# First modulation block requested earlier, convolution taps and small columns later, partial sums joined in PSUM, and each slab's matmuls issued in two halves

## The chip, the core and the metric

The kernel runs on one core of one Trainium2 chip. The time is that of the device in microseconds (us), from the first instruction of the program to the last; one launch does the whole computation. The engines named below are PE (TensorE matmuls; PEld is its weight load), DVE (VectorE), ACT (ScalarE), POOL (GpSimd) and SP (SyncE, which here only requests transfers). Each engine works through its own instructions in the order in which they stand in the program; a suffix q (SPq, ACTq) marks an engine's own queue handling, such as a request for a transfer.

## The reference, cut to what matters

One layer of a streaming encoder on x of shape 512 x 1024. What this study touches is the very beginning:

```
c_act = silu(c)                                   # c has 1024 numbers
mod   = c_act @ mod_w + mod_b                     # 1024 x 6144, split in six: sh1, sc1, g1, sh2, sc2, g2
h     = rms_norm(x, norm1_g) * (1 + sc1) + sh1    # 512 x 1024
proj  = h @ w_in                                  # 1024 x 8192, split among conv, HGRN2, stick-breaking, gates
```

Behind it come three branches (a causal convolution of 31 taps per channel, a gated linear recurrence, a stick-breaking attention), their gated sum, an output projection, a residual, and an MLP of width 4096 with squared ReLU. All inputs are float32.

## The kernel before, in words

Products are kept near float32 precision by splitting each operand in a high and a low part of the type float32r (`hilo`: ACT copies the high part, DVE subtracts it to get the low part) and by adding three matmuls (`mm3`, lines 113 to 115).

The first stage goes over the contraction dimension in eight steps j = 0 to 7, each for 128 rows of `w_in`. A step needs three things:

- **block(j)**, the tile `ms`: 128 columns of sc1 and 128 of sh1 from `mod_w`, 1 MB in two requests of 512 KB on SP (`load_ms`, line 130). `prep_mod` multiplies its eight row groups by c_act and adds them up in a tile `acc` of two halves: ACT makes the first product of each half (line 236), DVE adds the other six (line 238). For j > 0 DVE then joins the two halves (line 241); PE sums over the partitions with matmuls against a column of ones into the PSUM tile `tp` (line 245), and DVE makes from it the scale and shift of 128 channels (lines 247 and 248, the columns `modc`).
- **h(j)**: PE transposes 128 columns of the normalized x into the PSUM tile `tq` (line 254), ACT applies scale and shift (line 258, tile `s`) and copies the high part (line 83, tile `ht`), DVE makes the low part (line 84).
- **slab(j)**: 128 rows by 768 columns of `w_in` (`load_slab`, line 139), split into `fwh` and `fwl`.

Then `first_mm(j)` issues 18 matmuls into six PSUM tiles (`mm` and `f`), which are kept open over all eight steps. `prep(j)` stands ahead of `first_mm(j-1)` in the code.

Ahead of the loop, x comes in four tiles of 512 KB (line 143); each is squared and summed on ACT (line 88), and scaled by its reciprocal root on DVE (line 226). Small inputs come on ACT's queue: `vecs` (115 rows of 128 numbers: c, biases, gains) and `conv_w` (31 rows of 512, the **taps**), which PE transposes into columns (lines 170 and 175). Eight matmuls on constants (line 285) keep PE at work before the first real ones.

The order of the instructions on each engine is not that of the code: a scheduler, with its own estimate of how long things take, sets it when the program is built. `tc.issue_after(x)` forbids it to place what stands inside ahead of the instruction x.

Of the kernel before, what the change touches and what calls it, by code (L numbers as in the profile page):

```python
# [15 lines left out]
P = 128  # L16
# [5 lines left out]
CW = 31  # L22
# [16 lines left out]
def tile_hybrid_block(ctx, tc, x, vecs, mod_w, mod_b, w_in, conv_w, w_conv, w_hgrn, w_sb, w_out, w1, w2, out):  # L39
# [30 lines left out]
    def S(shape=(P, T), dt=F32, g=""):  # L70
        return spool.tile(list(shape), dt, name=TAG.get(g, "s"), bufs=BUFS.get(TAG.get(g)))
# [38 lines left out]
    def mm3(o, lhs, rhs, start, stop):  # L110
        lh, ll = lhs
        rh, rl = rhs
        TE.matmul(o, lhsT=lh, rhs=rh, start=start, stop=False)  # L113
        TE.matmul(o, lhsT=lh, rhs=rl, start=False, stop=False)  # L114
        TE.matmul(o, lhsT=ll, rhs=rh, start=False, stop=stop)  # L115


    vrow = S((NVEC, P), g="c0")
    A.dma_start(vrow, vecs)
    cw_row = S((CW, 512), g="c0")  # L120
    A.dma_start(cw_row, conv_w)
    x_v = x.rearrange("(a p) d -> a p d", p=P)
# [14 lines left out]
    def load_slab(j):  # L137
        slabs[j] = wpool.tile([P, W0], F32, name="slab", bufs=10)
        SY.dma_start(slabs[j], wi_row[:, j, C_A + 256:C_A + 256 + W0])

    for t in range(NT):
        xt.append(P4((P, D), g="x0"))
        SY.dma_start(xt[t], x_v[t])
    load_ms(0)
    load_slab(0)
# [26 lines left out]
    V.tensor_copy(vcol, vp[:, 0:NVEC])  # L172
    cp = ax()
    for i in range(4):
        TE.transpose(cp[:, i * 32:i * 32 + CW], cw_row[:, i * P:(i + 1) * P], ident[0:CW, 0:CW])
    cwc = C([P, 4, 32], F32)
    V.tensor_copy(cwc[:, :, 0:CW], cp[:, 0:128].rearrange("p (i k) -> p i k", k=32)[:, :, 0:CW])

    cact = C([P, 8], F32)
# [7 lines left out]
    oml = C([P, 4], F32)
    lb = vcol[:, V_HLB:V_HLB + 4]
    lbe = C([P, 4], F32)
    lbs = C([P, 4], F32)  # L190
    V.tensor_tensor(out=lbe, in0=lb, in1=lb, op=ALU.subtract)
    ph(lbe, lbe, AF.Exp)
    V.reciprocal(out=lbs, in_=lbe)
    V.tensor_tensor(out=lbe, in0=lbe, in1=lbs, op=ALU.mult)
    V.tensor_tensor(out=lbs, in0=lbe, in1=lbe, op=ALU.subtract)
    V.tensor_scalar(out=oml, in0=lbs, scalar1=-1.0, scalar2=1.0, op0=ALU.mult, op1=ALU.add)

    gbh = C([P, 24], F32)
    V.tensor_scalar(out=gbh, in0=vcol[:, V_GB:V_GB + 24], scalar1=0.5, scalar2=None, op0=ALU.mult)
    lnh = C([P, 8], F32)  # L200
    V.tensor_scalar(out=lnh, in0=vcol[:, V_LG:V_LG + 8], scalar1=0.5, scalar2=None, op0=ALU.mult)

# [7 lines left out]


    facc = [mm() if i < 4 else ps("f") for i in range(6)]
    hT, fw = [], {}

# [13 lines left out]
    def prep_mod(j):  # L228
        ms = ms_t.pop(j)
        acc = S((P, 2, 2, P), g="acc")  # L230
        for kk in range(KT):
            a, src, c = acc[:, kk % 2], ms[:, :, kk, :], cact[:, kk:kk + 1]
            if kk < 2 and j == 0:
                V.tensor_scalar(out=a, in0=src, scalar1=c, scalar2=None, op0=ALU.mult)
            elif kk < 2:
                A.activation(a, src, AF.Identity, scale=c)
            else:
                V.scalar_tensor_tensor(out=a, in0=src, scalar=c, in1=a, op0=ALU.mult, op1=ALU.add)
        ne = 2 if j == 0 else 1
        if ne == 1:  # L240
            V.tensor_tensor(out=acc[:, 0], in0=acc[:, 0], in1=acc[:, 1], op=ALU.add)
        tp = ps("tp")
        for q in range(2):
            for e in range(ne):
                TE.matmul(tp[:, q:q + 1], lhsT=acc[:, e, q, :], rhs=ones[:, 0:1], start=(e == 0), stop=(e == ne - 1))
        gs, sh = modc[:, j:j + 1], modc[:, 8 + j:9 + j]
        V.scalar_tensor_tensor(out=gs, in0=tp[:, 0:1], scalar=mb1[:, j:j + 1], in1=vcol[:, V_N1 + j:V_N1 + j + 1], op0=ALU.add, op1=ALU.mult)
        V.tensor_tensor(out=sh, in0=tp[:, 1:2], in1=vcol[:, V_MB + j:V_MB + j + 1], op=ALU.add)

    def prep_h(j):  # L250
# [17 lines left out]

    def prep(j):
        load_ms(j)  # L270
        load_slab(j)
        prep_mod(j)
        prep_h(j)
        prep_w(j)

    def first_mm(j):
        wh, wl = fw.pop(j)
        for i in range(6):
            c = slice(i * P, (i + 1) * P)
            mm3(facc[i], (wh[:, c], wl[:, c]), hT[j], j == 0, j == KT - 1)  # L280


    wu = ps("tq")
    for i in range(8):
        TE.matmul(wu, lhsT=ident, rhs=scanm.rearrange("p a t -> p (a t)"), start=True, stop=True)
    for t in range(NT):
        x_norm(t)
    prep_mod(0)
    prep_h(0)
    prep_w(0)  # L290
# [787 lines left out]
```

## Time and profile before

| | us |
|---|---|
| three runs, median (lowest to highest) | 924.02 (922.34 to 924.3) |
| the profiled execution, its own time | 924.09 |
| its span in the profile | 922.3 |
| first matmul of `first_mm(0)` begins | 25.06 |
| first matmul of step 4 begins | 47.13 |
| last matmul of step 7 begins | 65.79 |

The table's last three times count from the start of the span. PE is busy for 894.8 us of the 922.3. The busy time of PE is modelled (matmuls overlap), so a stretch with a full count can still hold short gaps.

### The profile page before, as it was taken

What the parts mean: (1) busy time and instruction counts of PE and PEld (TensorE: products, weight loads), DVE (VectorE), ACT (ScalarE), POOL (GpSimd) and SP (SyncE); (2) the same over time, 40 slices, a digit from 0 to 9 for tenths busy, and PEclk for the clock granted to TensorE, in tenths of its full rate; (3) what the DMA queues carried; (4) which work ended last, traced back from release to release, by engine and by line L of the source; (5) the groups of instructions that cost most, each with busy time, mean ns of one, the idle gap of its engine ahead of it and who ended that gap; (6) DMA issues with size and microseconds to landing.
All of it is one profiled execution on the core that took longest, in us unless ns stands there. A gap on an engine that the chain in (4) does not pass through costs nothing.

```text
span 922.3 us, 10624 instructions
## 1 busy us (share of the span) xinstructions
PE 894.8 (97%) x4185; PEld 728.8 (79%) x4185; DVE 599.5 (65%) x886; ACT 385.8 (42%) x596; POOL 28.1 (3%) x35
## 2 busy tenths in 40 slices
PE   4999989999988999999999999999999999999998
PEld 2788878888755588888888888888888888888886
DVE  4882388899999999997965544774423254442422
ACT  4652434475788632223833536453312123431210
POOL 1002000001032000000000000000000000000000
PEclk9999999999999999999999999999999999999999
DMA  9981301131200344793423620552242233142121
GB/s 279 279 268 59 113 12 46 52 132 46 91 1 1 115 159 162 245 329 136 138 86 103 216 70 1 192 196 91 92 137 92 56 113 106 46 137 92 68 69 46
DMA packets 85418, 107.78 MB, mean 117 GB/s; under 512 B 2270, under 2 KB 58705, under 8 KB 85368
## 3 DMA queue, kind: packets, MB, share of 16 engines
q1 hardware_dynamic: 85200, 106.96, 35.5%
q8 instruction: 33, 0.54, 0.3%
q14 instruction: 17, 0.14, 0.1%
q10 hardware_dynamic: 168, 0.14, 0.0%
HBM read 105.00 MB, written 2.10 MB: 116 GB/s over the span
## 4 chain that ended last, share of the span: by engine, by line
PE 88%; DVE 6%; ACT 3%; DMA 2%; issue 1%; SPq 1%; DVEq 0%; ACTq 0%
PE mm L113 14%; PE mm L114 14%; PE mm L115 14%; PE ax L115 9%; PE ax L113 9%; PE ax L114 9%; PE o L115 2%; PE o L114 2%; PE o L113 2%; PE g L113 2%; PE g L114 2%; PE g L115 2%; PE g L654 1%; DVE bt L545 1%; PE o L573 1%; DVE bt L546 1%
## 5 line engine op out<-in xcount | busy, mean ns | idle before, releaser
L84 DVE TENSOR_TENSOR wl<-w,wh 128x1024 fp32r<-128x1024 f32 x134 | 162.8, 1221 | 194.4 <-ACT wh L83 147.4
L83 ACT ACTIVATE wh<-w 128x1024 fp32r<-128x1024 f32 x134 | 139.8, 1054 | 290.8 <-PE ax L115 129.9
L113 PE MATMUL mm<-ht,wh 128*128 128x512 f32 x272 | 106.7, 392 | 0.0
L115 PE MATMUL mm<-ht,wl 128*128 128x512 f32 x272 | 106.6, 392 | 0.0
L114 PE MATMUL mm<-ht,wh 128*128 128x512 f32 x272 | 106.6, 392 | 0.0
L114 PE MATMUL mm<-p,wh 128*128 128x512 f32 (+1 forms) x272 | 102.6, 378 | 0.0
L115 PE MATMUL mm<-p,wl 128*128 128x512 f32 (+1 forms) x272 | 102.4, 377 | 0.0
L113 PE MATMUL mm<-p,wh 128*128 128x512 f32 (+1 forms) x272 | 102.3, 377 | 0.0
L462 DVE SCALAR_TENSOR_TENSOR cv<-cv,cbig 128x511 f32<-128x511 f32 (+29 forms) x120 | 83.5, 733 | 0.0
L113 PEld LDWEIGHTS mm<-ht,wh 128*128 128x128 f32 x272 | 51.1, 188 | 11.2 <-issue 0.8
L114 PEld LDWEIGHTS mm<-ht,wh 128*128 128x128 f32 x272 | 51.1, 188 | 11.0 <-issue 0.6
L115 PEld LDWEIGHTS mm<-ht,wl 128*128 128x128 f32 x272 | 51.1, 188 | 10.4 <-issue 0.2
L114 PEld LDWEIGHTS mm<-p,wh 128*128 128x128 f32 x272 | 51.2, 188 | 9.4
L115 PEld LDWEIGHTS mm<-p,wl 128*128 128x128 f32 x272 | 51.2, 188 | 9.4
L113 PEld LDWEIGHTS mm<-p,wh 128*128 128x128 f32 x272 | 51.0, 188 | 9.3
L113 PE MATMUL ax<-wh,p 128*128 128x512 f32 x128 | 49.8, 389 | 0.0
L114 PE MATMUL ax<-wl,p 128*128 128x512 f32 x128 | 49.8, 389 | 0.0
L115 PE MATMUL ax<-wh,p 128*128 128x512 f32 x128 | 49.8, 389 | 0.0
L113 PE MATMUL ax<-wh,s 128*128 128x512 f32 x128 | 49.8, 389 | 0.0
L114 PE MATMUL ax<-wl,s 128*128 128x512 f32 x128 | 49.8, 389 | 0.0
L115 PE MATMUL ax<-wh,s 128*128 128x512 f32 x128 | 49.8, 389 | 0.0
L865 DVE SCALAR_TENSOR_TENSOR s<-p,cbig,s 128x512 f32<-128x512 f32 x64 | 47.1, 746 | 1.5 <-DMA p<-in_mod_w_dram 1.2
(248 smaller groups left out, 1666.8 us busy)
## 6 DMA issues: line engine op xcount, KB each, us to landing
w<-in_w_dram SPq DMA_DIRECT2D x32, 1024.0 KB, 5.7
w<-in_w_in_dram SPq DMA_DIRECT2D x27, 1024.0 KB, 5.3
p<-in_mod_w_dram SPq DMA_DIRECT2D x32, 512.0 KB, 7.4
ms<-in_mod_w_dram SPq DMA_DIRECT2D x16, 512.0 KB, 5.9
w<-in_w_out_dram SPq DMA_DIRECT2D x4, 1024.0 KB
slab<-in_w_in_dram SPq DMA_DIRECT2D x8, 384.0 KB, 4.6
x<-in_x_dram SPq DMA_DIRECT2D x4, 512.0 KB, 8.9
w<-in_w_hgrn_dram SPq DMA_DIRECT2D x2, 1024.0 KB, 4.9
```

The lines of the kernel that those rows point to most:

```text
L83: A.activation(hi, src, AF.Copy)
L84: V.tensor_tensor(out=lo, in0=src, in1=hi.bitcast(F32), op=ALU.subtract)
L113: TE.matmul(o, lhsT=lh, rhs=rh, start=start, stop=False)
L114: TE.matmul(o, lhsT=lh, rhs=rl, start=False, stop=False)
L115: TE.matmul(o, lhsT=ll, rhs=rh, start=False, stop=stop)
L462: V.scalar_tensor_tensor(out=cacc[i][:, d:], in0=cu[i][:, 0:T - d], scalar=w, in1=cacc[i][:, d:], op0=ALU.mult, op1=ALU.add)
L545: V.tensor_tensor_scan(out=kp[:, 0:n][:, ::-1], data0=kp[:, 0:n][:, ::-1], data1=kp[:, 0:n][:, ::-1], initial=1.0, op0=ALU.mult, op1=ALU.b ...
L546: V.tensor_tensor(out=bt[:, 0:n - 1], in0=bt[:, 0:n - 1], in1=kp[:, 1:n], op=ALU.mult)
L573: TE.matmul(o[h * 64:h * 64 + 64, sb * P:T], lhsT=svt[sb][:, pr * P + h * 64:pr * P + h * 64 + 64], rhs=ahs[h][bi][:, off:off + n], start= ...
L654: TE.matmul(o[:, b * n:(b + 1) * n], lhsT=l, rhs=r, start=True, stop=True)
L865: V.scalar_tensor_tensor(out=a, in0=box["s"][:, kk, :], scalar=cact[:, 2 * k2 + kk:2 * k2 + kk + 1], in1=a, op0=ALU.mult, op1=ALU.add)
```

## The change

Five edits. `load_ms(0)` stands ahead of the requests for x in the code. The load of the taps, their transposes and the copy are put into `conv_columns`, called behind step 3's matmuls and not to be requested before line 265 of step 3 (`hb[3]`, the scale and shift of h(3)); other small columns are put into `lb_columns`, called behind step 1's. DVE no longer joins the halves of `acc` (line 241 is gone): PE adds both halves in PSUM, with four matmuls in place of two per step. `first_mm` is issued in two halves of three tiles, and `tp`, `tq` and all that follows for h(j) come between them, not to be issued before the first half has been. And `prep_w` comes ahead of `prep_h`.

```diff
-    cw_row = S((CW, 512), g="c0")
-    A.dma_start(cw_row, conv_w)
...
+    load_ms(0)
     for t in range(NT):
         xt.append(P4((P, D), g="x0"))
         SY.dma_start(xt[t], x_v[t])
-    load_ms(0)
     load_slab(0)
...
+    def conv_columns():
+        cw_row = S((CW, 512), g="c0")
+        with tc.issue_after(hb[3].ins):
+            A.dma_start(cw_row, conv_w)
+        cp = ax()
+        for i in range(4):
+            TE.transpose(cp[:, i * 32:i * 32 + CW], cw_row[:, i * P:(i + 1) * P], ident[0:CW, 0:CW])
+        V.tensor_copy(cwc[:, :, 0:CW], cp[:, 0:128].rearrange("p (i k) -> p i k", k=32)[:, :, 0:CW])
...
-        ne = 2 if j == 0 else 1
-        if ne == 1:
-            V.tensor_tensor(out=acc[:, 0], in0=acc[:, 0], in1=acc[:, 1], op=ALU.add)
+        return acc
+
+    def prep_sum(j, acc):
         tp = ps("tp")
         for q in range(2):
-            for e in range(ne):
-                TE.matmul(tp[:, q:q + 1], lhsT=acc[:, e, q, :], rhs=ones[:, 0:1], start=(e == 0), stop=(e == ne - 1))
+            for e in range(2):
+                TE.matmul(tp[:, q:q + 1], lhsT=acc[:, e, q, :], rhs=ones[:, 0:1], start=(e == 0), stop=(e == 1))
...
+    prep_sum(0, prep_mod(0))
     for t in range(NT):
         x_norm(t)
-    prep_mod(0)
+    prep_w(0)
     prep_h(0)
-    prep_w(0)
     for j in range(1, KT + 1):
         if j < KT:
-            prep(j)
-        first_mm(j - 1)
+            load_ms(j)
+            load_slab(j)
+            acc = prep_mod(j)
+            prep_w(j)
+        mid = first_mm(j - 1, range(3))
+        if j < KT:
+            with tc.issue_after(mid.ins):
+                prep_sum(j, acc)
+                prep_h(j)
+        first_mm(j - 1, range(3, 6))
+        if j == 2:
+            lb_columns()
+        if j == 4:
+            conv_columns()
```

What the scheduler makes of it at two places. **The start.** SP's first requests before (the four tiles of x are x_78 to x_84) and now (x_79 to x_85):

```order
L143 DMA x_78<-in_x_dram 128x1024
L143 DMA x_80<-in_x_dram 128x1024
L143 DMA x_82<-in_x_dram 128x1024
L143 DMA x_84<-in_x_dram 128x1024
L130 DMA ms<-in_mod_w_dram 128x8x128 x2
L139 DMA slab<-in_w_in_dram 128x768
```

```order
L142 DMA x_79<-in_x_dram 128x1024
L142 DMA x_81<-in_x_dram 128x1024
L142 DMA x_83<-in_x_dram 128x1024
L128 DMA ms<-in_mod_w_dram 128x8x128 x2
L142 DMA x_85<-in_x_dram 128x1024
L137 DMA slab<-in_w_in_dram 128x768
```

Block(0) has moved ahead of one tile of x, the last; three still stand ahead of it. On ACT, from the high part of slab(1) to that of slab(2), before (line 236 is a product of block(2), line 258 the scale and shift of h(0)) and now (lines 243 and 265):

```order
L83 ACTIVATE fwh<-slab 128x768
L258 ACTIVATE s<-tq,cbig 128x512
L236 ACTIVATE acc<-ms,cbig 128x256
L83 ACTIVATE ht<-s 128x512
L236 ACTIVATE acc<-ms,cbig 128x256
L83 ACTIVATE fwh<-slab 128x768
```

```order
L83 ACTIVATE fwh<-slab 128x768
L265 ACTIVATE s<-tq,cbig 128x512
L83 ACTIVATE ht<-s 128x512
L243 ACTIVATE acc<-ms,cbig 128x256 x2
L83 ACTIVATE fwh<-slab 128x768
```

The high part of h(0) no longer stands behind a product that needs block(2).

**Steps 3 and 4.** On ACT now, from the second product of block(5) ahead of h(3) on; the tile c_401 is the taps:

```order
L265 ACTIVATE s<-tq,cbig 128x512
L243 ACTIVATE acc<-ms,cbig 128x256
L83 ACTIVATE ht<-s 128x512
L83 ACTIVATE fwh<-slab 128x768
L100 ACT_TABLE_LOAD
L196 DMA c_401<-in_conv_w_dram 31x512
L243 ACTIVATE acc<-ms,cbig 128x256 x2
L265 ACTIVATE s<-tq,cbig 128x512
```

Before, the request of the taps was the second on ACT's queue (line 121), and no product stood between the lines 258 and 83 of h(1), h(2) or h(3), as line 243 does now in each. On PE now, from the sums of block(4) (which stand ten matmuls into step 3) to the first matmuls of step 4; line 199 transposes the taps:

```order
L252 MATMUL tp<-crs,acc 128x1 x4
L261 MATMUL tq<-crs,x_79 128x128
L261 MATMUL tq<-crs,x_81 128x128
L261 MATMUL tq<-crs,x_83 128x128
L261 MATMUL tq<-crs,x_85 128x128
L114 MATMUL mm<-ht,fwh 128x512
L115 MATMUL mm<-ht,fwl 128x512
L113 MATMUL f<-ht,fwh 128x512
L114 MATMUL f<-ht,fwh 128x512
L115 MATMUL f<-ht,fwl 128x512
```

```order
L113 MATMUL f<-ht,fwh 128x512
L114 MATMUL f<-ht,fwh 128x512
L115 MATMUL f<-ht,fwl 128x512
L199 MATMUL ax<-crs,c_401 128x31 x4
L113 MATMUL mm<-ht,fwh 128x512 x4
```

Behind the sums of block(4) come four transposes and eight matmuls of step 3, then the taps, then step 4. Before, the taps' transposes (line 175) were PE's second work, and the sums stood at the seam of two steps or a few matmuls into one. From the end of this stage on, all engines have the same instructions in the same order as before.

## Rows read from the trace of the kernel before

**Rows 1.** The page: busy time by engine (part 1), chain that ended last (part 4).

```profile
PE 894.8 (97%) x4185; PEld 728.8 (79%) x4185; DVE 599.5 (65%) x886; ACT 385.8 (42%) x596; POOL 28.1 (3%) x35
...
PE 88%; DVE 6%; ACT 3%; DMA 2%; issue 1%; SPq 1%; DVEq 0%; ACTq 0%
```

**Rows 2.** Stretches: length, PE, PEld, DVE, ACT, POOL busy, PE clock, DMA share, GB/s.

```profile
0.00:25.06 25.06, 11.49 (x37) 6.04 (x37) 11.48 (x38) 11.25 (x27) 3.70 (x17) 0.99 0.93 282
15.00:20.00 5.00, 5.00 (x14) 2.20 (x13) 5.00 (x14) 4.66 (x14) 0.00 (x0) 1.00 0.83 235
25.00:28.00 3.00, 2.94 (x8) 2.36 (x9) 1.43 (x3) 1.14 (x3) 0.00 (x0) 0.50 1.14 315
31.49:47.13 15.64, 15.64 (x85) 12.94 (x84) 14.89 (x38) 10.14 (x17) 0.00 (x0) 1.00 0.98 267
47.13:65.79 18.66, 18.62 (x91) 15.16 (x90) 17.42 (x44) 11.15 (x16) 0.00 (x0) 1.00 0.91 286
```

**Rows 3.** Chain that ended last, 25 to 66 us: shares by line.

```profile
by line: PE mm L113 21.4%; PE mm L114 18.7%; PE mm L115 18.5%; PE f L113 9.4%; PE f L115 8.9%; PE f L114 8.9%; PE tp L245 7.3%; PE tq L254 6.7%; ACT ht L83 1.3%; PE g L113 0.6%; issue 0.2%
```

**Rows 4.** Instructions in order of time, 0 to 25 us: start, length, ..., [idle before <-releaser].

```profile
0.73 0.56 ACTq L119 DMA_DIRECT2D c<-in_vecs_dram  x1
...
1.33 0.24 ACTq L121 DMA_DIRECT2D c<-in_conv_w_dram  x1
...
4.78 0.42 PE L170 MATMUL ax<-crs,c 115*128 115x115 f32 x1 [4.78 <-DMA c<-in_vecs_dram]
...
10.90 1.64 SPq L130 DMA_DIRECT2D ms<-in_mod_w_dram  x2
...
10.91 0.63 PE L175 MATMUL ax<-crs,c 31*128 31x31 f32 x4 [5.71 <-DMA c<-in_conv_w_dram]
...
14.43 0.35 DVE L234 TENSOR_SCALAR acc<-ms,cbig 128x256 f32<-128x256 f32 x1 [1.89 <-DMA ms<-in_mod_w_dram]
...
15.34 0.85 ACT L83 ACTIVATE fwh<-slab 128x768 fp32r<-128x768 f32 x1 [1.84 <-DMA slab<-in_w_in_dram]
...
19.88 0.95 PE L245 MATMUL tp<-crs,acc 128*128 128x1 f32 x8
...
22.71 0.78 ACT L258 ACTIVATE s<-tq,cbig 128x512 f32<-128x512 f32 x1 [2.04 <-DVE cbig L248]
...
23.98 0.51 ACT L236 ACTIVATE acc<-ms,cbig 128x256 f32<-128x256 f32 x1 [0.49 <-DMA ms<-in_mod_w_dram]
24.40 0.61 ACT L83 ACTIVATE ht<-s 128x512 fp32r<-128x512 f32 x1
...
25.06 2.07 PE L113 MATMUL mm<-ht,fwh 128*128 128x512 f32 x4 [2.63 <-ACT ht L83]
```

**Rows 5.** ACT's DMA queue, 5 to 6 us: packets, MB, share of 16 engines.

```profile
q10 hardware_dynamic: 4, 0.01, 2.1%
```

**Rows 6.** Instructions in order of time, steps 1 and 2 (columns as in Rows 4).

```profile
32.73 0.56 PE L245 MATMUL tp<-crs,acc 128*128 128x1 f32 x4
...
33.33 0.22 DVE L247 SCALAR_TENSOR_TENSOR cbig<-tp,cbig 128x1 f32<-128x1 f32 x1 [0.31 <-PE tp L245]
...
33.73 0.78 ACT L258 ACTIVATE s<-tq,cbig 128x512 f32<-128x512 f32 x1 [1.79 <-DVE cbig L248]
...
34.54 0.63 ACT L83 ACTIVATE ht<-s 128x512 fp32r<-128x512 f32 x1
...
39.46 1.28 ACT L100 ACT_TABLE_LOAD   x1
```

**Rows 7.** Groups by line, 31.45 to 61.65 us: busy us, mean ns | idle before.

```profile
L238 DVE SCALAR_TENSOR_TENSOR acc<-ms,cbig,acc 128x256 f32<-128x256 f32 x30 | 12.8, 478 | 0.0
...
L236 ACT ACTIVATE acc<-ms,cbig 128x256 f32<-128x256 f32 x8 | 3.6, 498 | 2.7 <-DMA ms<-in_mod_w_dram 2.7
L84 DVE TENSOR_TENSOR ht<-s,ht 128x512 fp32r<-128x512 f32 x5 | 3.5, 690 | 0.5 <-ACT ht L83 0.4
...
L241 DVE TENSOR_TENSOR acc<-acc 128x256 f32<-128x256 f32 x6 | 2.5, 418 | 0.0
```

More of the change, by code (lines that the diff above doesn't have):

```diff
@@ L114, in mm3 @@
         TE.matmul(o, lhsT=lh, rhs=rl, start=False, stop=False)
-        TE.matmul(o, lhsT=ll, rhs=rh, start=False, stop=stop)
+        return TE.matmul(o, lhsT=ll, rhs=rh, start=False, stop=stop)
     vrow = S((NVEC, P), g="c0")
     A.dma_start(vrow, vecs)
-    cw_row = S((CW, 512), g="c0")
-    A.dma_start(cw_row, conv_w)
     x_v = x.rearrange("(a p) d -> a p d", p=P)
@@ L172, in tile_hybrid_block @@
     V.tensor_copy(vcol, vp[:, 0:NVEC])
[L173 to L177, printed above, removed]
     cact = C([P, 8], F32)
@@ L184, in tile_hybrid_block @@
     V.tensor_tensor(out=cact, in0=vcol[:, V_C:V_C + 8], in1=ctmp, op=ALU.mult)
[L187 to L201, printed above, removed]
     mb_v = mod_b.rearrange("(o m) -> o m", o=1)
@@ L209, in tile_hybrid_block, with lb_columns @@
     modc = C([P, 16], F32)
+    cwc = C([P, 4, 32], F32)
+    oml = C([P, 4], F32)
+    gbh = C([P, 24], F32)
+    lnh = C([P, 8], F32)
+    hnh = C([P, 1], F32)
+    def conv_columns():
[6 more added lines that the diff above has]
+        V.tensor_copy(cwc[:, :, 0:CW], cp[:, 0:128].rearrange("p (i k) -> p i k", k=32)[:, :, 0:CW])
+    def lb_columns():
+        lb = vcol[:, V_HLB:V_HLB + 4]
+        lbe = C([P, 4], F32)
+        lbs = C([P, 4], F32)
+        V.tensor_tensor(out=lbe, in0=lb, in1=lb, op=ALU.subtract)
+        ph(lbe, lbe, AF.Exp)
+        V.reciprocal(out=lbs, in_=lbe)
+        V.tensor_tensor(out=lbe, in0=lbe, in1=lbs, op=ALU.mult)
+        V.tensor_tensor(out=lbs, in0=lbe, in1=lbe, op=ALU.subtract)
+        V.tensor_scalar(out=oml, in0=lbs, scalar1=-1.0, scalar2=1.0, op0=ALU.mult, op1=ALU.add)
+        V.tensor_scalar(out=gbh, in0=vcol[:, V_GB:V_GB + 24], scalar1=0.5, scalar2=None, op0=ALU.mult)
+        V.tensor_scalar(out=lnh, in0=vcol[:, V_LG:V_LG + 8], scalar1=0.5, scalar2=None, op0=ALU.mult)
+        V.tensor_scalar(out=hnh, in0=vcol[:, V_HN:V_HN + 1], scalar1=0.5, scalar2=None, op0=ALU.mult)
     facc = [mm() if i < 4 else ps("f") for i in range(6)]
-    hT, fw = [], {}
+    hT, fw, hb = [], {}, []
     def rstd_small(dst, ssq, n):
@@ L258, in prep_h @@
         b = A.activation(hf, tq, AF.Identity, scale=gs, bias=sh)
+        hb.append(b)
         if j == 3:
@@ L267, in prep_w, with first_mm @@
         fw[j] = (wh, wl)
[L269 to L278, printed above, removed]
+    def first_mm(j, tiles):
+        wh, wl = fw[j]
+        for i in tiles:
             c = slice(i * P, (i + 1) * P)
-            mm3(facc[i], (wh[:, c], wl[:, c]), hT[j], j == 0, j == KT - 1)
+            b = mm3(facc[i], (wh[:, c], wl[:, c]), hT[j], j == 0, j == KT - 1)
+        return b
     wu = ps("tq")
@@ L794, in conv_norm @@
             V.scalar_tensor_tensor(out=cacc[i], in0=th, scalar=1.0, in1=cacc[i], op0=ALU.add, op1=ALU.mult)
-    hnh = C([P, 1], F32)
-    V.tensor_scalar(out=hnh, in0=vcol[:, V_HN:V_HN + 1], scalar1=0.5, scalar2=None, op0=ALU.mult)
     for h in range(4):
```

## The prediction

> **What bounds the kernel now.** I read the page first, then the stretches, the chain of waits, and the instructions in order of time. On the page PE is busy for 97% of the span, and the chain that ended last runs over PE for 88% [rows 1]. So the question is what the change does to PE's timeline. From the end of the changed stage on (about 66 us) every engine has its old instructions in its old order; a shift that PE has there should reach the end whole.
>
> The stage falls in two parts. Up to 25.06 us PE has no real work: it is busy for 11.5 us of 25 and waits for data, the DMA being at 0.93 [rows 2]. From there to 65.79 the chain lies on PE: matmuls, the sums `tp` with 7.3% and the transposes `tq` with 6.7% of 41 us, but no line of DVE and only one short one of ACT [rows 3]. Per step that is 7.3% x 41 / 7 = 0.43 us for the sums and 0.39 for the transposes. The last four steps take 18.66 us [rows 2]; without three such pairs 16.2 are left for 72 matmuls, so 0.225 us for one.
>
> **The start.** PE, DVE and ACT each have the taps early in their order. The taps land at 10.91, though asked for at 1.33; `vecs`, of nearly the same size, lands at 4.78, and the taps take 6.1 us more [rows 4]. They move 4 packets in a microsecond, which is 2.1% of 16 engines, 0.34 of one, so 84 ns for each of the 31 rows: one at a time, on what looks like a single engine with other transfers in between [rows 5]. Since a load has landed only when its last engine is done, this engine also makes everything behind it late; and SP's second request of block(1) goes out at 10.90, as the taps land [rows 4].
>
> Two chains lead to the first matmul. DVE works from the landing of block(0) at 14.43, ACT from the landing of slab(0) at 15.34, both nearly without a gap (5.00 and 4.66 of 5 us) [rows 2, 4]. DVE's last scaling of x needs ACT's last root; then come the pair of columns and line 258 at 22.71.
>
> - Block(0) now stands behind three tiles of x, not four: 0.52 MB less at 282 GB/s [rows 2] is 1.8 us, and the taps are gone.
> - Slab(0) stands behind the same bytes as before. What was asked for ahead of it and itself is 3.6 MB, 12.8 us at that rate, against 15.34. If only the rate binds, it gains 2.5 us; if the taps never held it, nothing. I take the middle, 1.4, since the taps' engine is one of 16 but holds all landings.
>
> DVE gains about 1.8, ACT 1.4 plus the slack that DVE leaves it; I put line 258 1.8 us earlier. Behind it the high part of h(0) waited for a product of block(2), which landed at 23.98: it began at 24.40 instead of 23.49 [rows 4]. The new order takes this away: 0.9. **Start: -2.7 us** (between -0.9 and -3.4), first matmul at 22.4.
>
> The eight matmuls on constants no longer stand behind the taps and will be over early; PE is then idle until the first matmul. It starts at the lower clock level already now, 0.50 (1.2 GHz) for 3.0 us from 25 on [rows 2]. So no change; at most 1.5 us either way.
>
> **The steps.** *Sums.* Two more matmuls per step, and the chain paid 0.43 us for the two that it had; the eight passes of step 0 took 0.95 where four take 0.56 [rows 4, 6]. Seven steps: **+3.0** (2.6 to 3.3). The joins that go (seven of 0.42 on DVE [rows 7]) are not on the chain: nothing.
>
> *Taps on PE.* Four transposes of 0.63 us in all [rows 4], which lay in idle time, now lie between steps 3 and 4: **+0.5** (0.4 to 0.6).
>
> *Waits for h.* Before, the sums stood at the seam of two steps or just behind, a whole step ahead of the use of h(j). Now they come ten or more matmuls into the step. From the end of the sums to the high part of h it takes 33.29 to 35.17, 1.88 us [rows 6]; the product of the next block that now stands between the lines 265 and 83 adds 0.50 [rows 7]: 2.38. Behind the sums PE has 0.39 of transposes and six, eight or seven matmuls left in steps 0, 1 and 2: 1.74, 2.19 and 1.97. It waits 0.64, 0.19 and 0.41, together 1.2. From step 4 on no product stands between, and I count nothing. The low part of h follows on DVE (0.69) behind sums of the next block (0.43 each) that wait for ACT's second product; PE has four or five high matmuls (0.9 to 1.1) to cover this, and may lack 0.3 to 0.4 in three steps: 1.0 (0 to 1.3). Against this goes what the old order lost: three steps took 15.64 us where the pieces make 14.6 [rows 2], of which I let half go. **Waits: +1.7** (0 to +2.5).
>
> *The wait for the taps.* In their new place PE needs them ahead of step 4, and all later matmuls, h(5) to h(7) and DVE's copy stand behind. Count from the end of the sums of block(3). ACT needs 0.44 to line 265, then 0.78, a product 0.50, the high part 0.63, `fwh` 0.85, the table load 1.28 [rows 4, 6, 7]: the request goes out at +4.5. PE needs 2.38 to the start of step 3, ten matmuls 2.25, 0.35 for the low part, four sums 0.86, transposes 0.39, eight matmuls 1.8: it stands at the taps at +8.0. So a landing of up to 3.5 us costs nothing. The nearest rows are `vecs`, 4.05 us from request to landing, and the taps themselves, 9.58 [rows 4]; of the latter 3.4 lie behind `vecs` on the same queue. The DMA share in the steps is 0.98, like the 0.93 at the start [rows 2]. I take 6.5 (31 packets at 4 to 5 per microsecond): **+2.9** (0.5 to 6.0).
>
> The Trainium skill bears on this wait: by its page "DMA: Bandwidth & Descriptors", section "Why a DMA increments its semaphore by 16 and not by 1", a DMA is spread over the largest number of engines up to 16 that divides its row count. For 31 rows that is one engine, which is what [rows 5] look like. By the specifications on the same page, some 27 GiB/s per engine, an estimate for 63 KB is 2.2 us; the taps would then be there in time, the term 0, and the sum +2.5.
>
> Sum: -2.7 + 3.0 + 0.5 + 1.7 + 2.9 = **+5.4 us**. The profiled execution took 924.09 us (span 922.3), the median is 924.02, so they agree: 929.5.
>
> **Rivals.** (a) *The taps come in time*, within 3.5 us of the request. For it: little competes at that moment if SP has run dry. Against: neither transfer on ACT's queue did it. +2.5, so 926.6. (b) *Faster: DVE paces the steps.* It is busy 14.89 of 15.64 us there [rows 2], and the joins are 7 x 0.42 = 2.9 us. If PE's modelled busy time hides idle time that waits for DVE, the joins' 2.9 us come off and the added matmuls fall in gaps: -2.7 - 2.9 + 0.5 = -5.1, 919.0. It decides if the gaps are over 0.43 us per step; the chain of waits, with no DVE line, speaks against it. (c) *The change doesn't do what it says*: block(0) still goes behind three tiles of x, and if slab(0), behind the same bytes, lands at 15.34 as before, only the 0.9 us at h(0) is gained: 931.3. (d) *No new waits*: h is ready and the taps are there: -2.7 + 3.0 + 0.5 = +0.8, 924.9.
>
> **How the numbers follow.** Forecast 0.50, (a) 0.18, (b) 0.10, (c) 0.12, (d) 0.10. A measurement can tell about 0.2%, 1.9 us, from no change. Faster is (b), 0.10; within is (d) and the low edge of (a), 0.12; slower is the rest, 0.78. The range leaves out (b) and the upper end of (c): from (d) with the start at its best bound, 923.8, to the forecast with the taps at 9.6 us, 932.6.
>
> **What would show it.** In the new profile: the first `mm` matmul near 22.4, with no wait for the taps ahead of it; no ACT wait for block(2) ahead of `ht`; `tp` groups of eight passes at 0.86 us; short waits of PE for ACT's `ht` at steps 1 to 3; PE waiting for the DMA of `conv_w` near 47 us for some 3 us, DVE's copy behind it; the last matmul of step 7 near 71; the rest moved as one. I am wrong if the taps land within 3.5 us, if the first matmul comes before 21.5, or if PE shows gaps ahead of `tp` that the joins had made.

## The result, and the profile after

The changed kernel takes **930.72 us** (median of four runs, 928.25 to 932.09), the kernel before 923.18 (four runs, 921.95 to 924.3). The ratio is **1.0091**, with a 95% interval of 1.0075 to 1.0107: slower by 7.5 us, where +5.4 had been forecast. In later runs of both kernels it was 929.69 against 922.03, ratio 1.0088 (1.0073 to 1.0104). The profiled execution took 928.25 us, with a span of 926.1.

The page of the changed kernel, busy time by engine and the chain that ended last, against [rows 1]:

```profile
PE 900.4 (97%) x4213; PEld 731.2 (79%) x4213; DVE 598.2 (65%) x879; ACT 385.9 (42%) x596; POOL 28.1 (3%) x35
...
PE 87%; DVE 6%; ACT 4%; DMA 1%; issue 1%; SPq 1%; ACTq 0%; DVEq 0%
```

PE has 28 instructions more and DVE seven less, the joins. Nothing else on the page tells where the time went; the order of time does. The columns are those of [rows 4]:

```profile
5.30 9.41 PE L287 MATMUL tq<-cbig,crs 128*128 128x512 f32 x16
...
11.60 0.61 DVE L241 TENSOR_SCALAR acc<-ms,cbig 128x256 f32<-128x256 f32 x2 [4.84 <-DMA ms<-in_mod_w_dram]
...
13.80 0.84 ACT L83 ACTIVATE fwh<-slab 128x768 fp32r<-128x768 f32 x1 [5.17 <-DMA slab<-in_w_in_dram]
...
20.47 0.78 ACT L265 ACTIVATE s<-tq,cbig 128x512 f32<-128x512 f32 x1 [1.16 <-DVE cbig L255]
...
21.28 0.63 ACT L83 ACTIVATE ht<-s 128x512 fp32r<-128x512 f32 x1
...
21.96 2.08 PE L113 MATMUL mm<-ht,fwh 128*128 128x512 f32 x4 [2.06 <-ACT ht L83]
...
28.00 0.64 PE L261 MATMUL tq<-crs,x 128*128 128x128 f32 x4
...
30.47 1.20 PE L113 MATMUL mm<-ht,fwh 128*128 128x512 f32 x4 [0.45 <-ACT ht L83]
31.51 0.39 PE L114 MATMUL mm<-ht,fwh 128*128 128x512 f32 x1
...
32.88 0.95 PE L252 MATMUL tp<-crs,acc 128*128 128x1 f32 x8
...
33.69 0.64 PE L261 MATMUL tq<-crs,x 128*128 128x128 f32 x4
...
41.67 0.23 ACTq L196 DMA_DIRECT2D c<-in_conv_w_dram  x1
41.93 0.83 ACT L83 ACTIVATE fwh<-slab 128x768 fp32r<-128x768 f32 x1
42.08 1.20 PE L113 MATMUL mm<-ht,fwh 128*128 128x512 f32 x4 [0.22 <-ACT ht L83]
42.78 1.28 ACT L100 ACT_TABLE_LOAD   x1
...
48.88 0.40 PE L199 MATMUL ax<-crs,c 31*128 31x31 f32 x4 [1.09 <-DMA c<-in_conv_w_dram]
...
118.15 4.57 DVE L630 TENSOR_TENSOR_SCAN B<-cbig,B 128x512 f32<-128x512 f32 x4 [1.62 <-ACT B L88]
```

- Block(0) lands at 11.60 (14.43 before), slab(0) at 13.80 (15.34), the scale line at 20.47 (22.71). `ht` of h(0) follows it directly: the product of block(2) no longer stands between. PE's first matmul begins at 21.96 instead of 25.06 [rows 4], **3.1 us earlier**.
- The sums begin 0.81 us ahead of the transposes behind them (32.88 to 33.69), where the chain of before paid 0.43.
- PE waits for ACT's `ht` ahead of steps (0.45 and 0.22 in the rows shown), and for the taps ahead of 48.88; they were requested at 41.67, ahead of the high part of a slab (41.93) and of the table load (42.78), behind which the request stands in ACT's program.
- The transposes of h(1) run at 28.00, behind the sums of block(1). Before, they lay ahead of the first matmul (below).
- The last line is the first scan of the next stage on DVE. Before, it stands at 113.22 (below). I use it as the milestone for all experiments: the changed stage has moved it by **+4.93 us**.

The matmuls on constants are over at 14.7, and the stretches show what that did (length, PE, PEld, DVE, ACT, POOL busy, PE clock, DMA share, GB/s). Changed kernel:

```profile
15.00:21.96 6.96, 2.09 (x9) 1.01 (x8) 6.53 (x16) 5.65 (x14) 0.00 (x0) 0.63 1.14 320
21.96:27.00 5.04, 5.04 (x12) 3.98 (x13) 3.03 (x7) 1.75 (x3) 0.00 (x0) 0.50 1.16 314
...
47.63:48.88 1.25, 0.16 (x2) 0.03 (x1) 0.11 (x1) 0.43 (x1) 0.00 (x0) 1.00 1.08 340
...
51.00:54.00 3.00, 3.00 (x21) 2.70 (x20) 2.52 (x8) 0.96 (x2) 0.00 (x0) 1.00 0.97 313
```

Kernel before, the same view and some instructions:

```profile
15.00:25.06 10.06, 6.97 (x28) 3.70 (x26) 9.67 (x25) 7.20 (x18) 0.00 (x0) 0.98 0.98 281
...
124.00:126.00 2.00, 2.00 (x10) 1.25 (x9) 1.19 (x2) 0.00 (x0) 0.00 (x0) 0.50 0.02 4
```

```profile
20.68 0.52 PE L254 MATMUL tq<-crs,x 128*128 128x128 f32 x3
...
21.66 0.77 PE L254 MATMUL tq<-crs,x 128*128 128x128 f32 x5 [0.46 <-DVE x L226]
...
113.22 4.57 DVE L616 TENSOR_TENSOR_SCAN B<-cbig,B 128x512 f32<-128x512 f32 x4 [1.62 <-ACT B L88]
...
122.67 0.65 PE L650 MATMUL g<-tl 128*64 128x64 f32 x8 [2.32 <-DVE tl L677]
```

Between 15 us and its first real matmul PE was busy for 6.97 of 10.06 us before and is busy for 2.09 of 6.96 now. The first step then runs at the lower clock level (0.50, 1.2 GHz) for 5.04 us, where it was some 3.1 before [rows 2]; the mean of 0.63 ahead of it shows that the level had fallen before the step began. Two microseconds more at half speed are about **+1.0 us**. The eight transposes at 20.68 and 21.66 are those of h(0) and h(1): before, both lay in PE's idle time, now those of h(1) cost 0.39 us in the first step.

The stage's +4.93 ends as +3.8 in the span (926.1 against 922.3). The kernel before has a second stretch at 0.50 in this profile, from about 123.7 to 127, behind a wait of 2.32 us on PE; the changed kernel's profile has none there. This belongs to the execution, not to the change: another profile of the kernel before lacks it, and another of the changed kernel has it (below).

What PE and others wait for in the changed kernel, 25 to 72.5 us (us in total, times, longest):

```profile
PE ax L199 <- DMA c<-in_conv_w_dram: 1.1, 1, 1.1
...
PE mm L113 <- ACT ht L83: 0.7, 2, 0.4
PEld mm L114 <- DVE ht L84: 0.7, 2, 0.5
```

PEld's waits overlap PE's running matmuls in part. From PE's gaps in order of time, h costs 1.4 us ahead of the high parts (0.61, 0.15 and 0.38 at steps 1 to 3, 0.13 each at steps 5 and 7) and 0.3 at the low part of step 4. Something else comes with it. At the head of a step the four high matmuls take 1.04 us to the next one (30.47 to 31.51 above), where four such took 0.90 in a second profile of the kernel before:

```profile
60.08 1.07 PE L113 MATMUL mm<-ht,fwh 128*128 128x512 f32 x4
60.98 0.62 PE L113 MATMUL f<-ht,fwh 128*128 128x512 f32 x2
```

All of it lies between the first and the second of them, some 0.34 us instead of 0.23, in each of seven steps: 0.75 us, of a cause that no run here shows. The old order had gaps of its own beside its transposes, some 0.2 us, that are gone. Together 2.3.

| term | forecast | measured in the profile |
|---|---|---|
| start | -2.7 | -3.1 |
| clock of the first step | 0 (at most 1.5) | +1.0 |
| sums, 7 x (0.81 - 0.43) | +3.0 | +2.7 |
| transposes of the taps | +0.5 | +0.3 |
| transposes of h(1), in idle time before | not in the sum | +0.4 |
| waits for h | +1.7 | +2.3 |
| wait for the taps | +2.9 | +1.25 |
| sum, and the shift of the first scan | +5.4 | +4.85 of 4.93; 0.1 not assigned |

### The profile page after: what moved, and what is told of

Its sections match the earlier page's. It is cut to its first block, busy times and chain, and to the rows that moved or that the text cites. A ratio compares the mean times of both kernels' runs of the same rounds, so it can differ in the third digit from the quotient of the medians.

```text
span 926.1 us, 10689 instructions
## 1 busy us (share of the span) xinstructions
PE 900.4 (97%) x4213; PEld 731.2 (79%) x4213; DVE 598.2 (65%) x879; ACT 385.9 (42%) x596; POOL 28.1 (3%) x35
## 4 chain that ended last, share of the span: by engine, by line
PE 87%; DVE 6%; ACT 4%; DMA 1%; issue 1%; SPq 1%; ACTq 0%; DVEq 0%
PE mm L113 14%; PE mm L114 13%; PE mm L115 13%; PE ax L115 9%; PE ax L114 9%; PE ax L113 9%; PE o L115 2%; PE o L113 2%; PE o L114 2%; PE g L113 2%; PE g L114 2%; PE g L115 2%; PE g L668 1%; DVE bt L559 1%; PE o L587 1%
```

## The experiments

The theory was the table above: sums, waits for h and the taps cost more than the start gives. The rivals were that DVE paces the steps, that the taps' wait matters most, and later that the clock decides. All shifts are of the first scan against 113.22. That profile has a stretch at 0.50 in its first step; against the second profile of the kernel before (111.59), which has none, every shift is 1.63 higher, that of the changed kernel +6.56. The ratio is estimated from all runs of both kernels and is not the quotient of two medians. "Clock" is the mean granted clock of the profiled execution.

| kernel | median us | ratio (95%) | first matmul | shift | clock |
|---|---|---|---|---|---|
| changed | 930.72 | 1.0091 (1.0075 to 1.0107) | 21.96 | +4.93 | 0.994 |
| changed again | 929.69 | 1.0088 (1.0073 to 1.0104) | 22.00 | +6.73 | 0.990 |
| changed, joins on DVE | 925.03 | 1.0026 (1.0016 to 1.0036) | 22.26 | +1.01 | 0.994 |
| changed, taps behind step 7 | 927.03 | 1.0049 (1.0030 to 1.0067) | 21.81 | +4.23 | 0.992 |
| changed, PE kept busy at the start | 927.83 | 1.0064 (1.0047 to 1.0081) | 24.29 | +4.87 | 0.996 |
| before again | 922.34 | 1.0000 (0.9990 to 1.0010) | 25.05 | -1.63 | 1.000 |
| before, PSUM joins | 925.33 | 1.0037 (1.0024 to 1.0049) | 24.71 | +1.24 | 0.996 |
| before, halves | 927.55 | 1.0056 (1.0037 to 1.0076) | 24.79 | +2.59 | 0.998 |
| start alone | 923.73 | 1.0011 (1.0000 to 1.0022) | 21.41 | -1.55 | 0.992 |
| start, taps behind step 7 | 921.43 | 1.0000 (0.9989 to 1.0010) | 21.87 | -1.70 | 0.994 |
| the same, kept busy | 922.50 | 1.0009 (1.0000 to 1.0017) | 25.20 | -0.31 | 0.996 |
| the same, short work | 922.38 | 0.9998 (0.9987 to 1.0009) | 21.74 | -2.16 | 0.997 |
| the same, shorter work | 921.03 | 0.9992 (0.9982 to 1.0003) | 21.78 | -2.52 | 0.994 |

**The sums, undone.** The changed kernel with the joins on DVE again:

```diff
+        if j:
+            V.tensor_tensor(out=acc[:, 0], in0=acc[:, 0], in1=acc[:, 1], op=ALU.add)
         return acc
...
-            for e in range(2):
+            for e in range(1 if j else 2):
```

Expected: 

> The changed kernel with one thing undone: the partial sums of blocks 1 to 7 are joined on DVE again, so that PE runs two matmuls of one column per step instead of four. The shift of the stage is read at the first scan of the stage behind it, which starts at 113.22 us in the profile of the kernel before and at 118.15 in that of the changed one: +4.9. Theory (the sums cost what they occupy on PE, 0.81 us instead of 0.42 seven times, 2.7 us): the shift falls to about +2.2, and the time to some 2.7 us below the changed kernel. Rival (DVE paces the steps, so that the seven joins of 0.42 us come back on the path): the shift stays at +4.9 or above.

```profile
32.24 0.50 PE L254 MATMUL tp<-crs,acc 128*128 128x1 f32 x4
...
32.60 0.64 PE L263 MATMUL tq<-crs,x 128*128 128x128 f32 x4
```

In these rows of its order of time the sums take 0.36 us to the transposes instead of 0.81; seven times the difference is 3.15. The shift falls by 3.92, from +4.93 to +1.01, more than the 2.7 expected; of the rest some 0.5 is a shorter stretch at 0.50 (to about 26.3 instead of 27.0), 0.3 a shorter wait for the taps (0.97 instead of 1.25) and 0.3 smaller gaps, against a first matmul that comes 0.3 later. Runs of equal mean clock, 0.994, have medians of 925.27 and 929.06 us. With more work on DVE the kernel is faster, so DVE did not pace the steps: that rival falls.

**The sums alone**, in the kernel before:

```diff
-        ne = 2 if j == 0 else 1
-        if ne == 1:
-            V.tensor_tensor(out=acc[:, 0], in0=acc[:, 0], in1=acc[:, 1], op=ALU.add)
+        ne = 2
```

Expected: 

> The kernel before with one part of the change alone: the partial sums of blocks 1 to 7 are joined by PE, four matmuls of one column per step instead of two, and DVE's seven joins of 0.42 us go. Taps, start and the seams are as before, but three of the sums of block(1) now stand ahead of the first matmul. Theory (PE pays what the added matmuls occupy): each group of sums costs 0.81 us instead of 0.43, and the shift at the first scan is +2.2 to +3.2 at the same clock. Rival (DVE paces the steps): the joins' 2.9 us come off, and the shift is between -2.9 and 0.

```profile
24.12 0.73 PE L243 MATMUL tp<-crs,acc 128*128 128x1 f32 x6
...
30.51 0.95 PE L243 MATMUL tp<-crs,acc 128*128 128x1 f32 x8
31.32 0.64 PE L252 MATMUL tq<-crs,x 128*128 128x128 f32 x4
```

A miss: the shift is +1.24, below what was expected. Yet a group of sums has its full price here too, 0.81 us up to the transposes behind it (30.51 to 31.32), at the seam of two steps. What makes the shift small is in other places. The sums of block(1) have moved ahead of the first matmul (two passes at 23.52, six at 24.12), where PE waits anyway, so six groups are paid and not seven: 4.84 us in all against 2.97 for the seven of before, +1.9. The first matmul comes 0.35 earlier. And sums and transposes now stand together, where the old order broke the matmuls at two places in most steps; behind each break the first matmul takes 0.09 us more (28.28 to 28.59 in the kernel before, 0.31, where the next take 0.23). Breaks and gaps give back some 0.3 us: 1.9 - 0.35 - 0.3 = 1.25. What the joins on DVE had cost before is one wait of 0.2 us, among the waits of the kernel before from 25 to 68 us:

```profile
PEld tp L245 <- DVE acc L241: 0.2, 1, 0.2
```

**The halves alone**, in the kernel before, joins on DVE, order of the code `prep_mod`, `prep_w`, first half, sums and h, second half:

```diff
-            prep(j)
-        first_mm(j - 1)
+            load_ms(j)
+            load_slab(j)
+            acc = prep_mod(j)
+            prep_w(j)
+        mid = first_mm(j - 1, range(3))
+        if j < KT:
+            with tc.issue_after(mid.ins):
+                prep_sum(j, acc)
+                prep_h(j)
+        first_mm(j - 1, range(3, 6))
```

Expected: 

> The kernel before with one part of the change alone: block(j)'s sums and the transposes of h(j) come behind the first three tiles of a step. The joins stay on DVE, the taps and the order of the requests at the start are as before. Theory (h comes too late for the next step): the first matmul stays at 25.1 us, PE waits for ACT's and DVE's parts of h at the seams, and the shift at the first scan is +2.3 to +2.8. Rival (the waits for h in the changed kernel come from its other parts, the four sums and the taps): the shift is under +0.8.

Its waits, 25 to 72.5 us:

```profile
PE mm L113 <- ACT ht L83: 4.7, 4, 2.0
```

The 2.0 is the wait ahead of the first matmul; the others are 0.22, 1.44 and 1.03, together 2.7 us. The shift of +2.59 agrees with the expectation by its number, yet not wholly by its cause: this profile has no stretch at 0.50 at the start, which is worth 1.6 us (below), so against a kernel before without it the shift is 4.2. The two long waits stand ahead of steps 3 and 5 (42.34 and 53.78), where the scheduler put the high part of h behind the table load (40.36 to 41.64) and behind the high parts of a later weight tile and of a slab (51.43 to 53.21) on ACT. The halves are a loss in themselves, and their size hangs on ACT's order.

**The taps.** The changed kernel with the taps transposed behind step 7, requested as before:

```diff
+        with tc.issue_after(last_mm[0].ins):
+            for i in range(4):
+                TE.transpose(cp[:, i * 32:i * 32 + CW], cw_row[:, i * P:(i + 1) * P], ident[0:CW, 0:CW])
...
-        if j == 4:
+        if j == KT:
             conv_columns()
```

Expected: 

> The changed kernel with the four transposes of the taps queued on PE behind the last matmul of step 7; the request stays where it is. Theory (PE waits at step 4 for the taps and for nothing else that is as late): the 1.25 us of idle time ahead of the transposes go, but h(4) is ready only at about 48.1 us, 0.4 to 0.5 us behind the end of step 3, so the shift at the first scan falls from +4.9 to between +3.8 and +4.1. Rival (DVE or ACT set the pace of the steps, and the wait for the taps only covers another wait): the shift stays within 0.3 us of +4.9.

```profile
PEld mm L116 <- DVE ht L84: 1.0, 2, 0.8
```

No wait for the taps is left, but the shift falls by 0.70 only, not by the 1.25 of the wait, nor by the 0.8 to 1.1 expected: PE comes to h(5) earlier and waits for its low part (the row above; 0.6 us in order of time). Its other runs take 926.4 to 927.4 us, at mean clocks of 0.994 to 0.996; the changed kernel's have 0.990 to 0.994. At an equal 0.994 its two runs take 927.2 and 927.4 us, 1.7 less than the changed kernel's median of 929.06. So the taps' wait costs 0.7 us in the stage; where the other microsecond of these times lies, no profile shows.

**Both kernels again.** To see what differs between executions of one kernel, each was run again.

Expected: 

> The changed kernel once more, beside the kernels below, for a second profile and more times. So far its four executions took 928.25 to 932.09 us, and the fastest was the profiled one, with a mean granted clock of 0.994; the slowest two had 0.990. Theory (the times differ by how long the clock stays at 0.50, as those of the kernel before do, 920.5 to 921.3 us at a mean of 1.000 and 923.9 to 925.5 at 0.996): the shift at the first scan is again +4.5 to +5.5, the times fall in groups by the mean clock, and the median is 929 to 931 us. Rival (something else varies, such as the landing of the taps): the shift at the first scan itself moves by 2 us or more at the same clock.

Expected: 

> The kernel before once more, for a second profile. Its times so far fall in groups by the mean granted clock: 920.5 to 921.7 us at 0.999 and above, 921.3 to 923.2 at 0.998, 923.8 to 925.5 at 0.996; the profile shown had 0.996, with stretches at 0.50 from 24.7 to 28.1 us and near 124 us. Theory (each stretch at 0.50 under work costs 1.5 us, and whether it comes differs between executions): at 0.998 one of the two is missing in the new profile and the span is 920 to 921 us; at 1.000 both are, and it is about 919; at 0.996 the profile is as before. Rival (the groups come from something else and the clock only goes along): a profile at 0.998 or above with the same shares of the stage but another span.

Changed kernel, second profile, stretches:

```profile
47.00:49.06 2.06, 0.83 (x5) 0.37 (x3) 0.77 (x2) 1.95 (x4) 0.00 (x0) 1.00 1.08 326
...
51.00:54.00 3.00, 3.00 (x10) 2.42 (x10) 1.83 (x4) 0.00 (x0) 0.00 (x0) 0.50 0.86 292
129.00:132.00 3.00, 2.59 (x12) 2.21 (x13) 2.89 (x5) 1.09 (x2) 0.00 (x0) 0.57 0.00 0
```

Kernel before, second profile, the same:

```profile
25.00:28.00 3.00, 2.95 (x15) 2.49 (x16) 2.33 (x7) 1.63 (x3) 0.00 (x0) 1.00 1.15 313
122.00:132.00 10.00, 10.00 (x62) 8.44 (x61) 8.46 (x15) 3.18 (x3) 0.00 (x0) 1.00 0.01 2
```

The second profile of the changed kernel has a wait of 1.23 us for the taps, where the first has 1.09 in the same view, and then, about two microseconds later, a stretch at 0.50 that the first has not: its 3 us hold 10 matmuls, those of the first 21. Another lies near 129. The shift is +6.73, outside what was expected; the median and the groups by mean clock are as expected. The second profile of the kernel before has no stretch at 0.50 at either place, and its scan comes 1.63 us earlier (111.59) with the same work; its span is 919.1 against 922.3. So a stretch under full work costs about 1.6 us, and executions of one kernel differ by how many they have. The times follow: the kernel before, 920.3 to 921.7 us at a mean clock of 0.999 or 1.000, 921.8 to 923.2 at 0.998, 923.5 to 925.5 at 0.996; the changed one, 928.3 to 929.7 at 0.994, 931.2 at 0.992, 931.6 to 932.1 at 0.990. That the taps' wait causes the stretch behind it is argued from its place, and from the run without that wait; one of two profiles shows it, so it is not shown.

**The start alone.** Early block(0), late taps and columns, with the old order of the steps and joins on DVE. First with the taps transposed far behind the stage, then behind step 7:

```diff
+    load_ms(0)
     for t in range(NT):
...
         first_mm(j - 1, range(6))
...
+        if j == KT:
+            conv_columns()
```

Expected: 

> The start of the changed kernel alone: block(0) requested ahead of x, small columns later, the taps requested during the steps and transposed on PE a whole stage later, where PE waits anyway. Steps as before: joins on DVE, sums and transposes of h at the seams. Theory (the start is worth 3 us, of which the longer stretch at the lower clock takes 1 back): the first matmul at 22.0 to 22.5 us, the shift at the first scan -1.7 to -2.3, the time 0.15% to 0.25% below the kernel before. Rival (the steps wait for blocks that land no earlier than before, so what the start gains is lost by step 3): the first matmul as early, but a shift between -0.5 and +0.5.

Expected: 

> The start of the changed kernel with the old steps (joins on DVE, sums and transposes of h at the seams, whole steps); the taps are requested during the steps and transposed behind the last matmul of step 7. It is the earlier kernel with the start alone but for the place of these transposes, which there stood much later and moved the work behind the stage. Theory (the start is worth 3.6 us on PE, the longer stretch at the lower clock takes 1 back, the transposes 0.3): the first matmul at 21.4 us, the shift at the first scan -2.0 to -2.5, the shift at the end the same within 0.4 but for a low stretch near 124 us, the median 0.5 us above to 1.5 us below the kernel before, which often keeps its clock at the start. Rival (what the start gains is lost in the steps): a shift at the first scan above -1.

Stretches of the second of them:

```profile
15.00:21.87 6.87, 3.28 (x17) 2.12 (x16) 6.40 (x16) 5.51 (x14) 0.00 (x0) 0.66 1.11 319
21.87:27.00 5.13, 5.13 (x14) 4.26 (x15) 2.87 (x9) 2.45 (x4) 0.00 (x0) 0.50 1.15 314
```

Both first matmuls come over 3 us earlier and both scans only 1.55 and 1.70 earlier, less than expected: the stretch at 0.50 lasts 5 us. In the first kernel later work was re-ordered by the late transposes, its profile has a stretch at 0.50 from 297 us on, and the end came 0.23 later than before; its time was to be 0.15% to 0.25% lower and is not (ratio 1.0011). In the second the end came 3.0 earlier than in the first profile of before, but 0.1 later than in the second, which has no such stretch: 3.2 us earlier at the first matmul, 2.6 given back in clock and 0.4 for the taps' transposes. The times say the same: ratio 1.0000. By its mean clock (0.993 or 0.994) the kernel with the early start has its stretch in all twelve runs, the kernel before in some.

**PE kept busy up to the first matmul.** If idle time makes the clock fall, matmuls on constants put there should keep it up. In the changed kernel, and in the start with the taps behind step 7: four at the beginning, one behind the sums of block(0), one behind each transpose of h(0).

```diff
+    def keep(n, b):
+        with tc.issue_after(b.ins):
+            for i in range(n):
+                TE.matmul(facc[5], lhsT=ident, rhs=scanm.rearrange("p a t -> p (a t)"), start=True, stop=True)
...
             b = TE.transpose(tq[:, t * P:(t + 1) * P], xt[t][:, j * P:(j + 1) * P], ident)
+            if j == 0:
+                keep(1, b)
...
-    for i in range(8):
+    for i in range(4):
```

Expected: 

> The changed kernel with the matmuls on constants spread over PE's idle time: four instead of eight ahead of the first sums, one behind these, and one behind each of the four transposes of h(0). Nothing else is edited, but in ACT's order the table load and a product change places near step 4. Theory (the earlier first matmul finds the engine idle for longer, so that the clock stays at 0.50 for 5.1 us of the first step instead of 3.1, and this takes back 1 us or more of the start's 3): the first matmul at 21.9 to 22.3 us at a granted clock of 1.00, the first step 2.3 to 2.6 us shorter, the shift at the first scan +2.3 to +2.8, and the median 2 to 4 us below that of the changed kernel. Rival (the clock at the first step is not set by what PE did just before): the clock is 0.50 up to 26 us or later all the same, and the shift stays above +4.4.

Expected: 

> The start of the changed kernel with the old steps (joins on DVE, sums and transposes of h at the seams, whole steps), the taps requested during the steps and transposed behind step 7, and the matmuls on constants spread over PE's idle time at the start as in the kernel above. Theory (the start is worth 3.1 to 3.6 us, the clock gives back another 1.5, the taps cost 0.3): the first matmul at 21.4 to 22.0 us at a granted clock of 1.00, the shift at the first scan -3.8 to -4.8, and a time 0.25% to 0.5% below the kernel before. Rival (what the start gains is lost again in the steps or behind them, as in the kernel with the start alone, which was no faster than the kernel before): a ratio of 0.999 to 1.002.

Stretches of the first, and a few of its instructions:

```profile
15.00:19.00 4.00, 4.00 (x10) 2.34 (x11) 3.63 (x9) 3.89 (x12) 0.00 (x0) 0.50 1.15 318
24.29:27.00 2.71, 2.71 (x13) 2.21 (x13) 2.65 (x6) 1.48 (x3) 0.00 (x0) 1.00 1.12 329
```

```profile
15.91 2.05 PE L251 MATMUL f<-cbig,crs 128*128 128x512 f32 x2
...
24.29 1.21 PE L113 MATMUL mm<-ht,fwh 128*128 128x512 f32 x4 [0.73 <-ACT ht L83]
```

The first step now runs at full clock, as claimed. But both shifts miss (+4.87 and -0.31): the added matmuls themselves ran at 0.50 (2.05 us for one that takes two passes), the transposes of h(0) had to wait for them, and the first matmul came at 24.29 and 25.20. What the clock gave was lost by the displacement. The first kernel's median is 1.9 us below that of the changed kernel run again (927.83 and 929.69), near the 2 to 4 expected; the second is no faster than the kernel before.

**Shorter work in the gaps.** The start with the taps behind step 7 again, now with all eight matmuls at the beginning and shorter ones between the transposes of h(0): 256 columns, then 128.

```diff
+                TE.matmul(facc[5][:, 0:256], lhsT=ident, rhs=scanm.rearrange("p a t -> p (a t)")[:, 0:256], start=True, stop=True)
...
+            if j == 0:
+                keep(1 if t < 3 else 2, b)
```

Sums of block(1) come behind some matmuls of step 0, in the first kernel the transposes of h(1) too, and ACT's order at h(0) is held.

Expected: 

> The kernel with the start and the late taps, and work for PE in the idle time ahead of the first matmul again, but little of it: the eight matmuls on constants stay where they are, and one of 256 columns stands behind each of the first three transposes of h(0), two behind the fourth; the sums of block(1) and the transposes of h(1) follow the first matmuls. Theory (the clock falls since PE idles from 15.8 us on; short work there keeps it, if it displaces nothing): the first matmul at 21.4 to 22 us at a granted clock of 1.00, the shift at the first scan -3.3 to -4.5, a ratio of 0.996 to 0.9985. Rival (so little work doesn't hold the clock): 0.50 in the first step as without it, a shift of -1.5 to -2.5, a ratio of 0.999 to 1.001.

Expected: 

> As the kernel with the start and short work, but the matmuls on constants have 128 columns, ACT's order is that of the kernel with the start and the late taps, the transposes of h(1) stand ahead of the first matmul as there, and only the sums of block(1) wait for the first six matmuls. Theory A (the clock is worth its 1.5 to 2.5 us where the order of the other engines stays good): the first matmul at 21.4 to 22 us at 1.00, the shift at the first scan -3 to -4.5, a ratio of 0.996 to 0.9985. Theory B (with PE at full rate in step 0, ACT, DVE and the landing blocks set the pace, as in the kernel with short work, whose steps took 2.8 us longer than those of the kernel before at the same clock): the same clock and first matmul, but a shift of -1.5 to -2.5 and a ratio of 0.9985 to 1.001. Theory C (such short work doesn't hold the clock): 0.50 in step 0, as without it.

With 256 columns, stretches and instructions:

```profile
15.00:21.74 6.74, 4.25 (x23) 2.56 (x22) 6.33 (x16) 5.44 (x14) 0.00 (x0) 1.00 1.13 319
21.74:24.00 2.26, 1.76 (x6) 1.16 (x7) 2.23 (x7) 1.75 (x3) 0.00 (x0) 1.00 1.19 299
```

```profile
23.45 0.50 PE L117 MATMUL mm<-ht,fwh 128*128 128x512 f32 x1 [0.50 <-DVE ht L84]
...
26.42 0.51 ACT L248 ACTIVATE acc<-ms,cbig 128x256 f32<-128x256 f32 x1 [0.55 <-DMA ms<-in_mod_w_dram]
...
28.66 0.58 PE L264 MATMUL tp<-crs,acc 128*128 128x1 f32 x4 [0.47 <-ACT fwh L83]
```

Now the first matmul is at 21.74 and at full clock, 3.3 us earlier than in the second profile of before. The scan is only 0.53 earlier than there, and the shift, -2.16, misses its -3.3 to -4.5. PE, no longer held up by its clock, waits for DVE's low part, for ACT's `fwh`, and ACT for the next block: the steps take 2.8 us longer than in that profile, 0.8 of it transposes of h(1) and of the taps that lay ahead of the first matmul there. With 128 columns the profiled execution had 0.50 from about 18.6 to 25.4 (theory C), seven of the other eleven runs a mean clock of 0.996 or 0.998; its median, 921.03, is the lowest of all, but the interval takes in 1. No version is shown to be faster than the kernel before.

Moving the other small columns and putting `prep_w` ahead of `prep_h` were not run alone.

## Why the prediction was right, and where it was not

The direction and the place held: +7.5 us in the medians against +5.4, and +4.93 against +5.4 where the stage ends. That the sum came so near is in part luck: four of its terms were too high, by 2.5 us together (the taps' wait 1.65 of it), and three others too low or missing, by 2.0 (clock, waits for h, transposes of h(1)). Point by point:

- **The start**, -2.7, was -3.1: block(0) gained 2.8 us, not 1.8, slab(0) 1.5 (1.4 forecast), and the wait for block(2) is gone (0.9). Rival (c) falls.
- **The clock** is a step that failed: "So no change; at most 1.5 us either way". The text saw that the matmuls on constants would be over early and took the lower level as given; the rows of before only showed that it was at the lower level for 3.0 us in one execution. It costs 1.0 us more in the profiled execution, within that bound, but some 2.6 against an execution of the kernel before without the stretch. By the mean clocks the early start brings the stretch in every run, where the kernel before has it in some. The spans differ by 3.8 us between the first profiles of the two kernels and by 10.3 between the second (929.4 and 919.1); the medians' +7.5 lies between.
- **The sums**, +3.0, were +2.7, and 3.15 when undone. The mechanism stands: the full price, 0.81 us for eight passes, in the middle of a step and at a seam alike.
- **The transposes of h(1)** are in no term and in no rival. The change puts them behind the first half of step 0; before, they lay in idle time ahead of the first matmul. +0.4.
- **The waits for h**, +1.7, were 2.3. At steps 1 to 3 PE was to wait 0.64, 0.19 and 0.41 and waited 0.61, 0.15 and 0.38. Of the 1.0 for low parts only 0.3 came, at step 4; in its place stand 0.75 at the heads of steps and 0.26 at steps 5 and 7. The 0.5 set against them rests on a wrong reading: the stretch from 31.49 to 47.13 holds four groups of sums (32.73, 37.64, 41.82, 46.38) and not three, so 0.4 of the 1.04 us that it seemed to lose is a group. In the same way the 18.66 us behind it hold two pairs of sums and transposes and not three; a matmul takes 0.23 us, near enough to the 0.225 reckoned.
- **The wait for the taps** was mis-sized: 1.25 us, not 2.9. The landing took 7.2 us from the request (6.5 forecast), and PE stood at the taps 8.0 us behind the sums of block(3), as forecast. But the request went out 2.1 us behind these sums and not 4.5: ACT's queue made it at 41.67, while ACT had the high part of a slab and the table load still ahead of it, and both had been counted in. Without the wait only 0.7 us is gained in the stage, since h is late next. The estimate of 2.2 us from the figure per engine of the Trainium skill, page "DMA: Bandwidth & Descriptors", section "Specifications", doesn't hold for the time to landing here: 7.2 us, with the DMA share at 1.00 between request and landing; the measurement decides, and rival (a) falls. The taps' own packets took 3.5 us of engine time (4.0% of 16 engines over 5.5 us), and hardly any of them moved in the first 2 us.
- **Rival (b)**, DVE paces the steps, falls by the joins undone, and by the sums alone: seven joins fewer on DVE, and the kernel is slower. **Rival (d)**, no new waits, falls by the waits shown.
- "The rest moved as one" held within 0.5 us, but for stretches at 0.50 that differ between executions.

What decides in which executions the clock falls stays without a name.

## What to carry to other kernels

When a first matmul is moved forward, look at what PE does in the time ahead of it: here taking the taps away from the start let the matmuls on constants run early, which had kept PE busy up to the sums, and the 3 us gained were paid back in clock or, with the clock kept up, in waits for ACT, DVE and the next block. Extra passes on PE cost their full price in the middle of a step and at its seam (0.81 us for eight); they were free only ahead of the first matmul, where PE waits anyway. So ask also which work the new order takes out of idle time, as it did here with the transposes of h(1). And compare a change of under 1% by several profiles of each kernel, since one profile's clock can hide a third of it.

## What the runs showed of the hardware that was not expected

- Executions of one and the same kernel fall into groups some 1.6 us apart, told apart by the mean granted clock (920.3 to 921.7 us at 0.999 or 1.000, 921.8 to 923.2 at 0.998, 923.5 to 925.5 at 0.996).
- A wait of 1.2 us inside otherwise full work was followed by a stretch at 0.50 in one of two profiles of the same kernel. The wait of 2.3 us on PE in the stage behind the change (122.67 in the kernel before) stands in thirteen of the fourteen profiles, and a stretch at 0.50 follows it in eight of them.
- A transfer of 62 KB in 31 rows took 7.2 us from request to landing beside other traffic (DMA share 1.00, 308 GB/s), though nothing stood ahead of it on its queue; at the start it had taken 9.58 us behind another small load.
- ACT's queue made a request at 41.67 us that stands in ACT's program behind a copy that began at 41.93 and a table load that began at 42.78.
